# A rope half moved to VectorE, GpSimd's low weight parts cut in two, and eight products moved behind the last softmax steps

## The chip, the cores and the metric

The kernel runs on one core of one Trainium2 chip. A core has a matrix engine (TensorE, PE in the profile, with its weight loads as PEld), three engines for elementwise work (VectorE or DVE, ScalarE or ACT, GpSimd or POOL) and SyncE (SP), which here only issues DMAs. The metric is the device time of one execution in microseconds, taken as the median of several runs.

## The reference

Two layers over 1024 latent tokens of width 1024, with 256 context tokens beside them. All is float32.

```python
# layer 0: windowed attention, 16 query heads, 4 key/value heads of 128
proj = h_lat @ w_in                       # q | k | v | z
q, k = apply_rope(q), apply_rope(k)       # x1*cos - x2*sin, x2*cos + x1*sin
p = softmax([sink, q @ k_ctx.T, q @ k_window.T])   # window of +-128 tokens
y = ((p @ v) * silu(z)) @ w_out
x = x + gate * y
# layer 1: convolution branch, width 2048
a, gl, z = split(h @ w_in + b_in, 3)
u = depthwise_conv(a * sigmoid(gl), 31 taps) + b
y = (silu(layernorm(u)) * silu(z)) @ w_out
out = rmsnorm(x + gate * y) * final_g
```

Ahead of each layer stands a norm with a scale and a shift that are linear in silu(c).

## The kernel before

**High and low parts.** Each float32 product of the projections is made of three faster ones: both operands are split into a rounded high part and the rest, the low part, and high x high, high x low and low x high are added up in PSUM. The high part is a copy by ScalarE, the low part a subtraction (`split_lo`, line 163) by VectorE or GpSimd. A weight chunk is 128x1024: eight blocks of 128x128. The class `WStream` (line 219) loads the chunks in their order (`load`), splits them (`split`, line 239) and hands them out. There are two such streams: `wsA` (line 295) for the 40 chunks of the attention's input projection, `wsB` (line 1414) for the 48 of the convolution's. `wsB` is built with `hp=True`, so that its splits carry a high priority, and gives every low part that isn't VectorE's by a rule of its own (`lo_eng`) to GpSimd: 32 of 48. In `wsA` a low part by GpSimd is already made in two halves of 128x512.

**The order of the work.** TensorE runs its instructions in the order of the program; on the other engines a planner orders them by priority, which falls along the program, and by when it expects the inputs to be there. Each engine then works its queue strictly in order, and waits where an instruction's input is missing.

**The attention.** The softmax goes by pairs of heads and by steps: `steps` holds 8 pairs x 16 steps, a step being 64 queries of both heads. In step i TensorE makes the scores of step i+1 (`scores`, line 1140), then some products from a queue of other work (`fill`, line 1126), then the transposes of step i's probabilities (`transposes`, line 1185). Every fourth step adds products of probabilities with values (`pv`, line 1205). Between the scores and the transposes lie a masking reduction on VectorE, an exponential on ScalarE, a reciprocal on VectorE (tile `sc`) and a scaling on GpSimd (tile `p_page`). Transposed probabilities are split into high and low (tile `pt`) by ScalarE and VectorE.

What `fill` takes is generators of projections, each of which yields after every product: the other query heads and gates; first in the queue is head 1 of the queries (`second_q`, line 1090), last, in the final pair's steps from the eighth on, the first rows of the attention's output projection (`early_proj`, line 923: 7 rows x 2 token blocks x 6 products). `LAST_FILL` (line 40) says how many products a step of the final pair takes: the first number for its steps 0 to 7, the second for 8 to 15. After the last step a loop takes up to 12 more ahead of each product with values that is still due, and then all that is left (lines 1366 on). Before the first scores 18 and then 48 products have been taken, and so all 48 of `second_q`.

**The rope.** `rope` (line 951) takes a projected half of 512 tokens out of PSUM: a copy by ScalarE, two DMAs that swap its partition halves, a product with the cosine by VectorE, a product of the swapped copy with the sine, an addition, a high part by ScalarE and a low part. With `quick`, the sine product, and by `finish` (line 1005) also the addition and the low part, are VectorE's, else GpSimd's. `second_q` calls it for the query half 0 with `quick` and for the half 1 without. Half 0 serves the steps 0 to 7 of the first pair, half 1 the steps 8 to 15.

**Behind the attention.** `proj_attn` (line 761) multiplies by the output weights, in four quarters of the output; the last three rows of the last quarter go block by block, and each block is read out of PSUM by `evac0` (line 868) as soon as it is done: times the gate, plus x, the square's sum on ScalarE, the mean and its inverse root on VectorE (tiles `ms`, `sq`, `rr`, `rq`), scaling. Meanwhile the first chunks of `wsB` are split. In the convolution layer (`b_mm`, line 1647) TensorE makes the three projections; the 31 taps are shared between VectorE (even taps and sums) and ScalarE with GpSimd (odd taps). The layer's mean is a product with a tile of sums (`vsum_page`).

Of the kernel before, what the change touches and what calls it, by code (L numbers as in the profile page):

```python
# [18 lines left out]
KT = D // P  # L19
# [17 lines left out]
FIRST = 5  # L37
EARLY_ROWS = 7
EARLY_AT = 8
LAST_FILL = (11, 10)  # L40
FIRST_FILL = 48
KEEP = 8
BYBLOCK = 3
# [53 lines left out]
def backbone_kernel(  # L97
# [8 lines left out]
    V, A, G, PE, SY = (InOrder(tc, e) for e in (nc.vector, nc.scalar, nc.gpsimd, nc.tensor, nc.sync))  # L106
# [32 lines left out]
    def ps_g():  # L139
        return ps.tile([P, 512], F32, tag="g", name=nm("psg"), bufs=2)  # L140
# [13 lines left out]
    def act(out, in_, func, **kw):  # L154
        return A.activation(out=out, in_=in_, func=func, **kw)

    def tt(eng, out, a, b, op):
        return eng.tensor_tensor(out=out, in0=a, in1=b, op=op)

    def stt(out, in0, scalar, in1, op0, op1):  # L160
        return V.scalar_tensor_tensor(out=out, in0=in0, scalar=scalar, in1=in1, op0=op0, op1=op1)

    def split_lo(eng, lo, full, hi):
        return tt(eng, lo, full, hi.bitcast(F32), ALU.subtract)
# [54 lines left out]
    class WStream:  # L219
# [19 lines left out]
        def split(self, between=None):  # L239
            if self.ns >= self.nl:  # L240
                return
            i = self.ns
            r = self.raw.pop(i)
            h, l = pg.alloc(F32R, [KT, P], "whi"), pg.alloc(F32R, [KT, P], "wlo")
            if self.hp:
                with tc.high_priority():
                    act(h, r, AF.Copy)
                    split_lo(self.lo_eng(i), l, r, h)
            else:
                act(h, r, AF.Copy)  # L250
                if between:
                    between()
                if self.lo_eng(i) is G:
                    for a in range(0, KT, KT // 2):
                        split_lo(G, *(t[:, a:a + KT // 2] for t in (l, r, h)))
                else:
                    split_lo(self.lo_eng(i), l, r, h)
            pg.free(r)
            self.hl[i] = (h, l)
            self.ns += 1  # L260
# [147 lines left out]
    def ada_mm(kt):  # L408

        o = ps_o(0)[:, 0:256]  # L410
        for i in range(2):
            for k in range(4):
                PE.matmul(o[32 * k:32 * k + 32], c32[:, 4 * i + k, :], araw[kt][i][:, k], start=i == 0, stop=i == 1,
                          tile_position=(0, 32 * k))
        pg.free(*araw.pop(kt))
        if kt == KT - 1:
            pg.free(c32)
        return o
# [117 lines left out]
    o = ada_mm(0)  # L536
# [100 lines left out]
    def vt_split(vf, n, dh, dl):  # L637

        tp = ps_o(*vbank)
        for i in range(n // P):  # L640
            PE.transpose(tp[:, i * P:(i + 1) * P], vf[:, i * P:(i + 1) * P], ident)
        t3 = tp[:, 0:n].rearrange("p (a b) -> p a b", b=P)
        act(dh, t3, AF.Copy)
        split_lo(V, dl, t3, dh)
# [116 lines left out]
    def proj_attn():  # L761
# [38 lines left out]
        def ahead(i, nl, ns):  # L800
            while todo["load"] <= min(i + nl, len(seqB) - 1):
                load(todo["load"])
                todo["load"] += 1
            while todo["split"] <= min(i + ns, len(seqB) - 1):
                split(todo["split"])
                todo["split"] += 1
# [124 lines left out]
    qt = {}  # L931
    zt = {}

    def gemm_half(wc, half, o):
        wh, wl = wc
        sl = slice(half * 512, half * 512 + 512)
        for kt in range(KT):
            PE.matmul(o, wh[:, kt], Hh[kt][:, sl], start=kt == 0, stop=False)
            yield
            PE.matmul(o, wh[:, kt], Hl[kt][:, sl], start=False, stop=False)  # L940
            yield
            PE.matmul(o, wl[:, kt], Hh[kt][:, sl], start=False, stop=kt == KT - 1)
            yield

    def by_pairs(ap):
        return ap.rearrange("p (s t) -> p s t", t=64)

    def in_pair(page, n):
        return page.rearrange("p (s e t) -> p s e t", e=2, t=64)[:, :, n % 2]
# [55 lines left out]
    def finish(kind, n, half, o, d, ropes=None, hold=None, quick=False):  # L1005

        sl = slice(half * 512, half * 512 + 512)
        if kind in "kv" and half == 2:
            c = kvt[n][2]
            if kind == "k":  # L1010
                act(c[:, 0], o[:, 0:CT], AF.Copy)
                i = split_lo(V, c[:, 1], o[:, 0:CT], c[:, 0])
                while hold:
                    hold.pop()(i)
                return None
        if kind in "qk":
            return rope(o, sl, d, ropes, hold, V if quick or kind == "q" and half and n and n % 4 == 0 else G,
                        n if kind == "q" else None, quick)
        if kind == "z":
            dv, ov = in_pair(d, n), by_pairs(o)  # L1020
            anchor_z[:] = [act(dv, ov, AF.Tanh, scale=0.5), stt(dv, dv, 1.0, ov, ALU.add, ALU.mult)]
            return None
        w = CT if half == 2 else 512
        f = hp.alloc(F32, None, "vf")
        act(f[:, 0:w], o[:, 0:w], AF.Copy)

        def tail():
            if half == 2:
                vt_split(f, CT, *(c[:, i].rearrange("p (a b) -> p a b", b=P) for i in (2, 3)))
            else:  # L1030
                vt_split(f, 512, *(t[:, half * 4:half * 4 + 4] for t in d))
            hp.free(f)

        return tail
# [50 lines left out]
    def split_next(i):  # L1085
        if wsA.ns <= i:
            wsA.split()
            wsA.load()

    def second_q():  # L1090
        i = cidx[("q", 1)]
        wc = wsA.need(i)
        wsA.load()
        for half in range(2):
            o = ps_g()
            yield from gemm_half(wc, half, o)
            if half == 0:
                split_next(i + 1)
            finish("q", 1, half, o, qt[(0, half)], quick=half == 0)
        wsA.done(i)  # L1100

    def pair_job(kind, pr, half):
# [203 lines left out]
    def next_pv():  # L1306
        pr, qq = pvq.popleft()
        fill(1000, ("z", pr, qq // 2))
        pv(pr, qq)

    fillq.append(("q1", second_q()))
    enqueue_pairs(0)
    fill(18)
# [6 lines left out]
    for i, (pr, st) in enumerate(steps):  # L1320
        h, qb = 2 * pr + st // 8, st % 8
# [15 lines left out]
        if not regroup:  # L1337
            n = 15 if pr and pr % 2 == 0 and st < 4 and not final else LAST_FILL[st // 8] if final else FILL - (i < 6)
            if pr // 2 in vlate and pr:
# [667 lines left out]
```

## Time and profile before

| What | Value |
|---|---|
| median of the runs | 1678.72 us |
| runs | 1678.7 to 1679.17 us |
| the profiled execution | 1680.83 us |
| its span, first to last instruction | 1679.1 us |
| granted TensorE clock, mean | 0.999 |
| busy: TensorE, VectorE, ScalarE, GpSimd | 1666.0, 1091.2, 870.2, 874.9 us |

The profile is of one execution, which is a little longer than the runs; it is read for where time lies, and a difference found in it is applied to the median. A row of the timeline reads: start and duration in us, engine, instruction, output<-inputs by the tiles' names, shape, count, and in brackets how long the engine had stood before it and what ended that. A count over 1 means that alike neighbours were merged into one row, whose duration is theirs together. TensorE's products overlap: one that is listed with 0.39 us lets the next start 0.23 us behind it, so that a stall is read from the starts. A row of the grouped view gives the count, then the busy time of all in us and the mean of one in ns, then the idle time ahead of them. All instructions of the kernel carry the line of a helper (L91), so the tiles tell them apart.

### The profile page before, as it was taken

Reading aid. Unit: us, or ns where it says so; the run is one execution under the profiler, and the core shown is the slowest. Engines: PE = TensorE matmul, PEld = TensorE weight load, DVE = VectorE, ACT = ScalarE, POOL = GpSimd, SP = SyncE. Lnnn points to the kernel's source line nnn. Section 1 sums busy time; section 2 is a strip of 40 time slices with the busy share of each in tenths; the row PEclk is TensorE's granted clock in tenths of the full one; section 3 lists DMA queues with packets and bytes.
Section 4 is the critical chain, followed back from the end, with each engine's and each line's share of the span. In section 5 each row is a group of like instructions: output and inputs, shape, how many; then the busy total and the mean of one; then the engine's idle time right before and its main releaser. Section 6 shows DMA issues by size and latency. Waiting matters only on the chain.

```text
span 1679.1 us, 23843 instructions
## 1 busy us (share of the span) xinstructions
PE 1666.0 (99%) x8340; PEld 1396.3 (83%) x8340; DVE 1091.2 (65%) x2063; ACT 870.2 (52%) x1523; POOL 874.9 (52%) x831
## 2 busy tenths in 40 slices
PE   9999999999999999999999999999999999999998
PEld 6888888888888888888888788888888888888886
DVE  5755554555455554556234389999999999868832
ACT  5644543555355544546333365555665664566731
POOL 0246673576547564642001268999898887130400
PEclk9999999999999999999999999999999999999999
DMA  9424442444335443457976522020211212387981
GB/s 382 171 62 144 141 144 76 142 154 151 105 125 167 148 129 98 127 159 262 325 247 215 193 88 101 1 76 14 76 50 51 88 38 70 132 276 246 318 288 50
DMA packets 139607, 244.63 MB, mean 146 GB/s; under 512 B 44650, under 2 KB 61346, under 8 KB 139488
## 3 DMA queue, kind: packets, MB, share of 16 engines
q1 hardware_dynamic: 133408, 233.15, 40.7%
q10 hardware_dynamic: 6080, 9.97, 2.4%
q8 instruction: 65, 1.06, 0.2%
q14 instruction: 54, 0.44, 0.1%
HBM read 190.90 MB, written 41.69 MB: 139 GB/s over the span
## 4 chain that ended last, share of the span: by engine, by line
PE 97%; DVE 1%; DMA 1%; POOL 0%; ACT 0%; issue 0%; ACTq 0%; POOLq 0%; DVEq 0%
PE psg L91 50%; PE pss L91 26%; PE pso L91 22%; DMA rope_half<-rope_half 1%; POOL rope_half L91 0%; DVE rq L91 0%; DVE x_page L91 0%; DVE ms L91 0%; DVE rope_half L91 0%; POOL kl_page L91 0%; DVE wlo_page L91 0%; ACT whi_page L91 0%; ACTq L91 0%; ACT rope_half L91 0%; DVE hf_page L91 0%
## 5 line engine op out<-in xcount | busy, mean ns | idle before, releaser
L91 POOL TENSOR_TENSOR odd_half<-odd_half,prod_half 128x513 f32<-128x513 f32 (+2 forms) x252 | 314.5, 1256 | 22.5 <-ACT prod_half L91 9.2
L91 POOL TENSOR_TENSOR wlo_page<-wraw_page,whi_page 128x512 fp32r<-128x512 f32 (+1 forms) x104 | 174.9, 1698 | 157.2 <-ACT whi_page L91 125.7
L91 PE MATMUL psg<-hh_page,whi_page 128*128 128x512 f32 x600 | 236.8, 395 | 0.0
L91 PE MATMUL psg<-hl_page,whi_page 128*128 128x512 f32 x600 | 234.8, 391 | 0.0
L91 PE MATMUL psg<-hh_page,wlo_page 128*128 128x512 f32 x600 | 234.3, 390 | 0.0
L91 ACT ACTIVATE prod_half<-ubuf,dww 128x513 f32<-128x513 f32 (+2 forms) x252 | 165.6, 675 | 116.7 <-POOL odd_half L91 113.0
L91 PE MATMUL psg<-h2h_page,whi_page 128*128 128x512 f32 x464 | 181.9, 392 | 0.0
L91 PE MATMUL psg<-h2h_page,wlo_page 128*128 128x512 f32 x464 | 180.6, 389 | 0.0
L91 PE MATMUL psg<-h2l_page,whi_page 128*128 128x512 f32 x464 | 180.6, 389 | 0.0
L91 DVE SCALAR_TENSOR_TENSOR pss<-ubuf,dww,pss 128x512 f32<-128x512 f32 (+3 forms) x270 | 173.0, 674 | 0.1
L91 DVE SCALAR_TENSOR_TENSOR pss<-ubuf,wsum,pss 128x512 f32<-128x512 f32 (+3 forms) x270 | 172.3, 674 | 0.2
L91 ACT ACTIVATE pt<-pss 128x640 fp32r<-128x640 f32 (+1 forms) x128 | 86.7, 677 | 142.5 <-PE pss L91 142.5
L91 POOL TENSOR_SCALAR p_page<-p_page,sc 128x576 f32<-128x576 f32 (+2 forms) x128 | 93.2, 728 | 106.9 <-DVE sc L91 104.4
L91 ACT ACTIVATE p_page<-p_page,sc 128x577 f32<-128x577 f32 (+2 forms) x128 | 96.9, 757 | 78.6 <-DVE sc L91 76.7
L91 DVE CUSTOM_DVE_ANT_0 p_page<-pss,mask_page,nsink 128x576 f32<-128x576 f32 (+1 forms) x112 | 90.2, 806 | 70.5 <-PE pss L91 57.4
L91 PEld LDWEIGHTS psg<-hh_page,wlo_page 128*128 128x128 f32 x600 | 112.7, 188 | 24.2
L91 PEld LDWEIGHTS psg<-hh_page,whi_page 128*128 128x128 f32 x600 | 112.7, 188 | 19.7 <-ACT hh_page L91 0.3
L91 PEld LDWEIGHTS psg<-hl_page,whi_page 128*128 128x128 f32 x600 | 113.0, 188 | 19.1 <-DVE hl_page L91 0.2
L91 DVE TENSOR_TENSOR pt<-pss,pt 128x640 fp32r<-128x640 f32 (+1 forms) x128 | 100.7, 787 | 36.3 <-ACT pt L91 36.1
L91 ACT ACTIVATE whi_page<-wraw_page 128x1024 fp32r<-128x1024 f32 x88 | 92.6, 1052 | 53.9 <-PE psg L91 19.3
L91 PE MATMUL pso<-h2h_page,whi_page 128*128 128x512 f32 x304 | 118.3, 389 | 0.0
L91 PE MATMUL pso<-h2l_page,whi_page 128*128 128x512 f32 x304 | 118.3, 389 | 0.0
(255 smaller groups left out, 3915.6 us busy)
## 6 DMA issues: line engine op xcount, KB each, us to landing
wraw_page<-in_k_wconv_dram SPq DMA_DIRECT2D x48, 512.0 KB
wraw_page<-in_k_win_dram SPq DMA_DIRECT2D x40, 512.0 KB
wo_page<-in_attn_w_out_dram SPq DMA_DIRECT2D x32, 512.0 KB
wol_page<-wolA SPq DMA_DIRECT2D x32, 512.0 KB
wo_page<-in_conv_w_out_dram SPq DMA_DIRECT2D x32, 512.0 KB
wol_page<-wolC SPq DMA_DIRECT2D x32, 512.0 KB
rope_half<-rope_half ACTq DMA_DIRECT2D x76, 128.0 KB
araw_page<-in_k_ada_dram SPq DMA_DIRECT2D x16, 512.0 KB
```

Of the source, the lines that this page charges most:

```text
L91: r = f(*a, **k)
```

## The change

Three places. The second half of head 1's rope is called with `quick=True` too, so that its sine product, its addition and its low part are VectorE's. In streams with `hp=True`, which is `wsB` alone, a low part by GpSimd is made by two instructions of 128x512 instead of one of 128x1024; those by VectorE stay whole. In the final pair's steps 8 to 15, `fill` is asked for 9 products instead of 10.

```diff
@@ -37,7 +37,7 @@
-LAST_FILL = (11, 10)
+LAST_FILL = (11, 9)
@@ -245,7 +245,9 @@
             if self.hp:
                 with tc.high_priority():
                     act(h, r, AF.Copy)
-                    split_lo(self.lo_eng(i), l, r, h)
+                    n = KT // 2 if self.lo_eng(i) is G else KT
+                    for a in range(0, KT, n):
+                        split_lo(self.lo_eng(i), *(t[:, a:a + n] for t in (l, r, h)))
@@ -1096,7 +1098,7 @@
             yield from gemm_half(wc, half, o)
             if half == 0:
                 split_next(i + 1)
-            finish("q", 1, half, o, qt[(0, half)], quick=half == 0)
+            finish("q", 1, half, o, qt[(0, half)], quick=True)
```

## The prediction

> **What bounds the kernel now.** I read the page's head and its chain by engine first, then TensorE's rows in order of time for every place where two products start further apart than they need to, then the rows of the other engines around those places.
>
> ```profile
> span 1679.1 us, 23843 instructions
> PE 1666.0 (99%) x8340; PEld 1396.3 (83%) x8340; DVE 1091.2 (65%) x2063; ACT 870.2 (52%) x1523; POOL 874.9 (52%) x831
> PE 97%; DVE 1%; DMA 1%; POOL 0%; ACT 0%; issue 0%; ACTq 0%; POOLq 0%; DVEq 0%
> 1023.81 5.44 PE pso L91 x24
> ```
>
> TensorE is busy for 99% of the span and holds 97% of the chain. The last row, from the chain, gives the pace of an undisturbed 128x512 product: 5.44/24 = 0.227 us. The change takes no product away, so all that it can win is time in which TensorE stands. Three such places lie where the change works; I call them A, B and C. A is the first softmax step:
>
> ```profile
> 94.35 0.39 PE L91 MATMUL psg<-hl_page,whi_page 128*128 128x512 f32 x1
> 96.31 0.66 PE L91 MATMUL pss<-ident,p_page 128*128 128x128 f32 x4 [1.58 <-POOL p_page L91]
> ...
> 93.00 1.29 POOL L91 TENSOR_TENSOR rope_half<-rope_half,sin_page 128x512 f32<-128x512 f32 x1 [5.92 <-DMA rope_half<-rope_half]
> 94.38 1.27 POOL L91 TENSOR_TENSOR rope_half<-rope_half,rope_half 128x512 f32<-128x512 f32 x1
> 95.62 1.31 POOL L91 TENSOR_SCALAR p_page<-p_page,sc 128x448 f32<-128x448 f32 x2
> ...
> 88.04 0.69 DVE L91 TENSOR_TENSOR rope_half<-rope_half,rope_half 128x512 f32<-128x512 f32 x1
> 91.56 0.68 DVE L91 CUSTOM_DVE_ANT_1 p_page<-pss,mask_page,nsink 128x448 f32<-128x448 f32 x1 [0.84 <-PE pss L91]
> 93.25 0.17 DVE L91 RECIPROCAL sc<-sc 128x1 f32<-128x1 f32 x1 [0.22 <-ACT p_page L91]
> 96.83 0.69 DVE L91 SCALAR_TENSOR_TENSOR zs_page<-zs_page,psg 128x512 f32<-128x512 f32 x1 [2.71 <-ACT zs_page L91]
> ...
> 90.51 2.36 DMA rope_half<-rope_half
> ```
>
> TensorE could have gone on at 94.35 + 0.23 = 94.58 and goes on at 96.31: it stands for 1.73 us. The transposes wait for GpSimd's scaling of the first probabilities. Its factor is there at 93.42 (the reciprocal), but GpSimd's queue holds the rope of head 1's second query half ahead of it, which waits for a transfer that lands at 92.87 and then takes two additions' time, to 95.65.
>
> B is the end of the attention's output projection:
>
> ```profile
> 959.84 0.39 PE L91 MATMUL pss<-woh_page,ozl_page 128*128 128x512 f32 x1
> 961.25 0.50 PE L91 MATMUL pss<-woh_page,ozh_page 128*128 128x512 f32 x1 [1.01 <-DVE x_page L91]
> ...
> 952.69 7.68 POOL L91 TENSOR_TENSOR wlo_page<-wraw_page,whi_page 128x1024 fp32r<-128x1024 f32 x3 [28.89 <-DMA wraw_page<-in_k_wconv_dram]
> ...
> 952.83 2.82 DVE L91 TENSOR_TENSOR x_page<-x_page,xr_page 128x512 f32<-128x512 f32 x1
> 956.44 1.49 DVE L91 SCALAR_TENSOR_TENSOR ms<-ssf 128x1 f32<-128x1 f32 x1 [0.79 <-ACT junk_half L91]
> 958.40 2.00 DVE L91 SCALAR_TENSOR_TENSOR rq<-rr 128x1 f32<-128x1 f32 x1
> 960.43 0.16 DVE L91 TENSOR_TENSOR rq<-rq,ms 128x1 f32<-128x1 f32 x1
> 960.50 0.69 DVE L91 TENSOR_TENSOR x_page<-pss,gate_page 128x512 f32<-128x512 f32 x1
> ...
> 955.68 0.63 ACT L91 ACTIVATE junk_half<-x_page 128x512 f32<-128x512 f32 x1 [1.79 <-DVE x_page L91]
> 956.31 1.05 ACT L91 ACTIVATE whi_page<-wraw_page 128x1024 fp32r<-128x1024 f32 x1
> ```
>
> Here TensorE stands for 961.25 - 959.84 - 0.23 = 1.18 us, until VectorE has read block 1 out of PSUM (960.50). That read sits in VectorE's queue behind block 0's norm, and three instructions of that norm are swollen: the addition takes 2.82 where the rope's of the same shape takes 0.69, and two instructions on a single column take 1.49 and 2.00 where their sibling takes 0.16. GpSimd runs three whole low parts just then, 952.69 to 960.37, some 2.5 us each, and the swollen instructions end at 955.65, 957.93 and 960.40, about where a third of that row does each time.
>
> C is the last softmax step, before its value products:
>
> ```profile
> 798.81 0.60 PE L91 MATMUL pss<-ident,p_page 128*128 128x128 f32 x4
> 800.18 0.47 PE L91 MATMUL pso<-pt,kvc_page 128*128 128x512 f32 x1
> 800.88 1.43 PE L91 MATMUL pso<-pt,kvc_page 128*128 128x512 f32 x5 [0.23 <-DVE pt L91]
> ...
> 799.50 0.60 ACT L91 ACTIVATE pt<-pss 128x512 fp32r<-128x512 f32 x1 [2.22 <-PE pss L91]
> 800.13 0.69 DVE L91 TENSOR_TENSOR pt<-pss,pt 128x512 fp32r<-128x512 f32 x1 [2.12 <-ACT pt L91]
> ```
>
> TensorE stands for 800.88 - 800.18 - 0.23 = 0.47 us for the low part of the transposed probabilities. A, B and C together are 3.38 us: the most that I can name.
>
> **The rope on VectorE.** Three instructions leave GpSimd (sine product, addition, low part) for VectorE, which does the first half's addition in 0.69. They add 2.07 us to an engine that idles for 2.71 just behind. No DMA is added; the swap is issued by ScalarE as before. The products of this half are first read eight steps later, so only what the three displace counts. Where they stand in VectorE's queue isn't in the trace. If the two reciprocals keep their place, scaling starts at 93.45, ends at 94.1 (half of 1.31), before TensorE wants it: gain 1.73. If, as on GpSimd today, product and addition stand ahead of the reciprocal, they run 92.9 to 94.3; reciprocal to 94.5, scaling to 95.15, TensorE at 95.2: gain 1.1. If the product stands ahead of the score reduction, VectorE waits for the landing with the reduction behind it, which then starts at 94.3 instead of 91.56; reduction to scaled probabilities takes 91.56 to 93.42 plus 0.65 = 2.5, so TensorE goes at 96.85: a loss of 0.5. I take 1.1, because on GpSimd the addition was put ahead of the scaling. Next late would be the second step's scaling, which the last GpSimd row (x2) shows right behind the first and which moves forward with it.
>
> **The halves.** 32 low parts of 128x1024 become 64 of 128x512. The grouped rows give both shapes:
>
> ```profile
> L91 POOL TENSOR_TENSOR wlo_page<-wraw_page,whi_page 128x512 fp32r<-128x512 f32 x72 | 94.9, 1341 | 90.1 <-ACT whi_page L91 89.2 <-POOL p_page L91 0.5 <-PE pss L91 0.3
> L91 POOL TENSOR_TENSOR wlo_page<-wraw_page,whi_page 128x1024 fp32r<-128x1024 f32 x32 | 80.1, 2504 | 67.1 <-ACT whi_page L91 36.5 <-DMA wraw_page<-in_k_wconv_dram 28.9 <-PE psg L91 1.7
> ```
>
> GpSimd pays 2 x 1.341 - 2.504 = 0.18 us more for each, 5.7 in all; no weight is waited for at B or behind it, so that lies beside TensorE's work. At B I replay the queue with halves of 1.25. The addition (issued 952.83) gets through at 953.94 and ends at 954.55, 1.1 sooner. Square and its sum on ScalarE to 955.35; the mean waits for the second half, done by 955.95; the root stands behind a weight copy of 1.05 on ScalarE, 956.65; the reciprocal to 956.85; the next instruction waits for the third half, done 957.35; its successor, free today, may be caught by the fourth, done 958.75. Block 1 is then read by 959.45, and TensorE wants the bank at 960.07: all of 1.18 goes, with 0.6 to spare. If mean and both that follow are each caught for a whole half (1.25 + 0.16), they end at 956.75, 958.65 and 960.1, block 1 is read by 960.8 and 0.5 is won; and if the last one is caught by the very last half, which may end at 961.4 (the present 960.37 with three extra costs of 0.18 and the addition's share let in), B costs up to 1 us more than now. I take 1.18, since the first term alone nearly covers it. The Trainium skill ("SBUF — State Buffer", section "Who interferes with whom") says that a VectorE instruction with two SBUF inputs and a GpSimd instruction that reads SBUF exclude each other for the whole instruction, by order of issue. By that rule twice as many GpSimd instructions are twice as many chances to be caught, and B would give the 0.5; the swollen rows agree that a wait ends with GpSimd's instruction, and show three caught beside three low parts.
>
> **Nine early products.** Eight steps give up one product each; the early projection has 7 rows x 2 blocks x 6 = 84 products, so 72 stand in the steps (80 before) and 12 behind the last transposes (4 before), which is what the closing loop takes at once. At C the transposes start at 798.81 and the low part is done at 800.82, 2.0 later. From the transposes to the first value product lie 1.37 with four products, 0.91 of it theirs; with twelve it is 0.46 + 12 x 0.227 = 3.2: covered, 0.47 won. The price is 0.23 us less cover in each of the steps. Only one has as little:
>
> ```profile
> 780.19 0.75 POOL L91 TENSOR_SCALAR p_page<-p_page,sc 128x576 f32<-128x576 f32 x1 [1.67 <-DVE sc L91]
> 781.18 0.71 PE L91 MATMUL pss<-ident,p_page 128*128 128x128 f32 x5
> ```
>
> 780.94 against 781.18: 0.24 of cover for 0.23. I cost it at nothing; if the order there is worse, up to 0.4 stays behind.
>
> The sum: 1.1 + 1.18 + 0.47 = 2.75, near 2.8. The profiled execution took 1680.83, its span is 1679.1, so 1.7 lies around it, untouched; 1680.83 - 2.8 = 1678.0. The median, 1678.72, is 2.1 lower than that execution, and the gain is one of stalls that each execution should have: 1678.72 - 2.8 = 1675.9.
>
> **The rivals.** First, all three stalls go in full: 3.38, 1675.3. For it: VectorE's idle 2.71 behind the reciprocals; against it, GpSimd's order today.
>
> Second, the rope blocks VectorE ahead of the first score reduction: -0.5 + 1.18 + 0.47 = 1.15, 1677.6. For it, the product ranks ahead of the scores in the program's order; against it, the reduction is ready at 91.56, well before the landing.
>
> Third, the halves don't do what they are there for, because as many of VectorE's small instructions are caught: 1.1 + 0.47 = 1.6, 1677.1.
>
> Fourth, slower. In the convolution both engines are nearly full and VectorE's last sum is only just in time, as the timelines and the grouped rows of that stage show:
>
> ```profile
> 1432.59 0.69 DVE L91 TENSOR_TENSOR vsum_page<-vsum_page,v_page 128x512 f32<-128x512 f32 x1
> 1434.38 1.02 PE L91 MATMUL pso<-vsum_page,ones 128*128 128x512 f32 x2
> ...
> L91 DVE TENSOR_TENSOR wlo_page<-wraw_page,whi_page 128x1024 fp32r<-128x1024 f32 x13 | 20.4, 1572 | 5.4 <-ACT whi_page L91 4.5 <-issue 0.5
> L91 DVE TENSOR_TENSOR vsum_page<-vsum_page,v_page 128x1024 f32<-128x1024 f32 x13 | 20.4, 1570 | 0.0
> ...
> 1023.68 1.23 DVE L91 TENSOR_TENSOR wlo_page<-wraw_page,whi_page 128x1024 fp32r<-128x1024 f32 x1
> ```
>
> The sum ends at 1433.28, TensorE reads it at 1434.38: 1.1 us of cover at the end of the whole stage. VectorE's 26 wide instructions with two SBUF inputs already take 0.34 longer than a free one (1.57 against 1.23), 8.9 us. Were more GpSimd instructions to double that, VectorE would be 8.9 - 1.1 = 7.8 late there: 1678.72 - 2.8 + 7.8 = 1683.7. It decides from 1.1 us on. Against it: low parts are few beside the odd taps' additions on GpSimd, and each is caught for less time once it is short.
>
> **How the numbers follow.** Forecast 0.45, all in full 0.22, rope ahead of the reduction 0.13, halves without effect 0.12, convolution late 0.08. A measurement here can tell about 0.2% from no change, 3.4 us, so faster means under 1675.4: the case in full (0.22), and some of the forecast's (0.06), 0.28. Slower is the fourth rival and a little of the unknown at B, 0.09; the rest, 0.63, is within. The range goes from 1675.3 less the 0.5 by which the runs shown differ, 1674.8, to 1677.6 plus the same, 1678.1; the slow case is left out.
>
> **What would show it.** A: transposes of the first step at 95.2 (forecast) or 94.6, no rope of that half on GpSimd at 93, and the reciprocal behind or ahead of the addition on VectorE. B: the 2.82, 1.49 and 2.00 each shorter by a microsecond, and no wait in the last block of the projection. C: 12 products between the last transposes and the value products, and no wait there. The convolution: the last sum still ahead of TensorE's mean. The forecast is wrong if a new wait of over 0.5 us stands in the softmax steps from the eighth of the last pair on, or at the mean.

## The result, and the profile after

| | before | after |
|---|---|---|
| median | 1679.05 us (8 runs) | 1683.51 us (8 runs) |
| ratio | 1 | 1.0027, 95% interval 1.0016 to 1.0038 |
| the profiled execution | 1680.83 us, span 1679.1 | 1682.3 us, span 1680.2 |
| mean granted TensorE clock | 0.999 in the profiled execution | 0.996 to 0.999 |

The three runs behind the 1678.72 of before are among its eight here. The granted clock is the share of its full speed that TensorE is given. The changed kernel is slower by 4.5 us; the forecast was 2.8 us faster, with a range that ended at 1678.1. The busy times on the page after, and its chain by engine:

```profile
PE 1665.3 (99%) x8340; PEld 1395.6 (83%) x8340; DVE 1088.1 (65%) x2066; ACT 869.7 (52%) x1523; POOL 876.1 (52%) x860
PE 95%; DMA 2%; DVE 1%; POOL 1%; ACT 1%; issue 0%; ACTq 0%; POOLq 0%; DVEq 0%; SPq 0%
```

TensorE is as busy as before (1665.3 against 1666.0), and TensorE's share of the chain falls from 97% to 95%: the time is lost in stands. The rows of the timeline after that answer to those of A:

```profile
93.51 0.39 PE L91 MATMUL psg<-hl_page,whi_page 128*128 128x512 f32 x1
97.17 0.65 PE L91 MATMUL pss<-ident,p_page 128*128 128x128 f32 x4 [3.27 <-POOL p_page L91]
...
92.02 0.69 DVE L91 TENSOR_TENSOR rope_half<-rope_half,sin_page 128x512 f32<-128x512 f32 x1 [2.24 <-DMA rope_half<-rope_half]
92.75 0.69 DVE L91 TENSOR_TENSOR rope_half<-rope_half,rope_half 128x512 f32<-128x512 f32 x1
93.36 0.68 DVE L91 CUSTOM_DVE_ANT_1 p_page<-pss,mask_page,nsink 128x448 f32<-128x448 f32 x1
96.21 0.16 DVE L91 RECIPROCAL sc<-sc 128x1 f32<-128x1 f32 x1 [0.89 <-ACT p_page L91]
...
93.47 0.63 ACT L91 ACTIVATE qh_page<-rope_half 128x512 fp32r<-128x512 f32 x1 [4.44 <-DVE rope_half L91]
94.12 1.28 ACT L91 ACT_TABLE_LOAD   x1
95.41 0.67 ACT L91 ACTIVATE p_page<-p_page,sc 128x449 f32<-128x449 f32 x1
...
96.47 1.39 POOL L91 TENSOR_SCALAR p_page<-p_page,sc 128x448 f32<-128x448 f32 x2 [10.31 <-DVE sc L91]
```

A is twice as long: 97.17 - 93.51 - 0.23 = 3.43 us for 1.73. GpSimd is free now and scales at once, but its factor comes at 96.37. VectorE's queue holds the sine product ahead of the first score reduction and waits 2.24 us in it for the swapped copy; the product and the addition then go first, and the reduction starts at 93.36, though its scores were there from about 90.7 (91.56 before, and TensorE is 0.84 earlier here, 93.51 for 94.35). On ScalarE the high part of the rope stands ahead of the load of the exponential's table. The timeline of before has that load in an idle time, and the rope's high part behind the exponentials:

```profile
91.15 1.28 ACT L91 ACT_TABLE_LOAD   x1 [1.18 <-issue]
92.45 0.67 ACT L91 ACTIVATE p_page<-p_page,sc 128x449 f32<-128x449 f32 x1
95.68 0.63 ACT L91 ACTIVATE qh_page<-rope_half 128x512 fp32r<-128x512 f32 x1 [1.76 <-POOL rope_half L91]
```

So the exponential starts 2.05 us behind the reduction now (95.41 - 93.36), and before 0.89 (92.45 - 91.56).

The rows that answer to B and C, and one place that is new:

```profile
955.14 0.69 DVE L91 TENSOR_TENSOR x_page<-x_page,xr_page 128x512 f32<-128x512 f32 x1
957.28 0.98 DVE L91 SCALAR_TENSOR_TENSOR ms<-ssf 128x1 f32<-128x1 f32 x1 [1.44 <-ACT junk_half L91]
959.65 1.11 DVE L91 SCALAR_TENSOR_TENSOR rq<-rr 128x1 f32<-128x1 f32 x1
960.68 0.68 DVE L91 TENSOR_TENSOR x_page<-pss,gate_page 128x512 f32<-128x512 f32 x1
...
798.83 0.60 PE L91 MATMUL pss<-ident,p_page 128*128 128x128 f32 x4
801.83 0.39 PE L91 MATMUL psg<-woh_page,ozl_page 128*128 128x512 f32 x1
802.05 1.52 PE L91 MATMUL pso<-pt,kvc_page 128*128 128x512 f32 x6
...
813.92 0.39 PE L91 MATMUL pss<-woh_page,ozl_page 128*128 128x512 f32 x1
815.25 0.68 PE L91 MATMUL pso<-ident,dwr_page 32*128 32x32 f32 x8 [0.94 <-DVE dww L91]
```

B's wait is gone: block 1 is read at 960.68 and no product of the last block waits. Of the three swollen instructions the last two are shorter (0.98 and 1.11 for 1.49 and 2.00), but the first, the addition, isn't caught at all, that is, it doesn't wait for GpSimd: 0.69, not a shortened 2.82. The two shorter ones are not the halves' doing either: in a run further down that has whole low parts and an addition that isn't caught (e8) they take 0.83 and 0.96. So this trace doesn't show yet what the halves do. C is gone: the value products follow 0.22 us behind the last of the twelve. One place is worse: at 815.25 TensorE stands for 1.1 us (815.25 - 813.92 - 0.23) at the transposes of the convolution's taps, where before it didn't. The chain of waits after says why:

```profile
799.50 13.09 DMA ozf_page<-ozd
812.68 1.07 ACT ozh_page L91
813.77 1.23 DVE ozl_page L91
```

VectorE's copy of the first taps, whose bank the next transposes need, stands in its queue behind the low part of the last attention rows (the row DVE ozl), whose transfer lands at 812.6. Before, that transfer was issued at the same time (799.47), and ScalarE's high part of it started at 807.82 instead of 812.68.

Of the profiled executions, then: A 1.7 worse, B 1.18 and C 0.47 better, the taps 1.1 worse. That is about what the spans differ by (1.1), and not the 4.5 of the medians. The mean clocks say that something is missing: this profiled execution, at 0.999, is the fastest of the eight; four of the eight have a mean clock of 0.997 or less. Of the 127 runs of before that stand beside the experiments two have: one at 0.997, and one that took 2078 us and, like one of e3's and one of e7's at over 4300 us, enters no ratio.

### The profile page after: what moved, and what is told of

The parts are those of the page before. It is cut to its first block, busy times and chain, and to the rows that moved or that the text cites. A ratio compares the mean times of both kernels' runs of the same rounds, so it can differ in the third digit from the quotient of the medians.

```text
span 1680.2 us, 23876 instructions
## 1 busy us (share of the span) xinstructions
PE 1665.3 (99%) x8340; PEld 1395.6 (83%) x8340; DVE 1088.1 (65%) x2066; ACT 869.7 (52%) x1523; POOL 876.1 (52%) x860
## 3 DMA queue, kind: packets, MB, share of 16 engines
q8 instruction: 65, 1.06, 0.3%
## 4 chain that ended last, share of the span: by engine, by line
PE 95%; DMA 2%; DVE 1%; POOL 1%; ACT 1%; issue 0%; ACTq 0%; POOLq 0%; DVEq 0%; SPq 0%
PE psg L91 49%; PE pss L91 25%; PE pso L91 21%; DMA rope_half<-rope_half 1%; DMA ozf_page<-ozd 1%; DMA wolA<-low_page 1%; POOL rope_half L91 0%; POOL low_page L91 0%; ACT whi_page L91 0%; DVE rope_half L91 0%; ACTq L91 0%; POOL p_page L91 0%; ACT rope_half L91 0%; ACT qh_page L91 0%; DVE x_page L91 0%
## 5 line engine op out<-in xcount | busy, mean ns | idle before, releaser
L91 POOL TENSOR_TENSOR wlo_page<-wraw_page,whi_page 128x512 fp32r<-128x512 f32 x136 | 180.2, 1347 | 154.2 <-ACT whi_page L91 122.8
```

The costliest lines, as they stand in the source:

```text
L91: r = f(*a, **k)
```

## The experiments

Theory Q: the rope's place in the queues of VectorE and ScalarE is the loss. The first rival was that the nine products, through the taps' transposes, or the halves cost as much. (The expectations of e1 to e4 call the theory R and this rival Q; from e5 on the theory is Q.) Every kernel was timed beside runs of before; the medians of before lie between 1679.72 and 1679.80.

| kernel | median, us | ratio to before, 95% interval | stand at A in its trace |
|---|---|---|---|
| rope alone (e1) | 1683.80 | 1.0021, 1.0012 to 1.0030 | 3.68 |
| halves alone (e2) | 1679.62 | 0.9998, 0.9989 to 1.0007 | 1.92 |
| nine alone (e3) | 1679.85 | 1.0001, 0.9992 to 1.0010 | 1.92 |
| halves and nine, no rope (e4) | 1679.78 | 1.0001, 0.9992 to 1.0010 | 1.50 |
| rope alone, behind the softmax (e5) | 1678.27 | 0.9990, 0.9981 to 0.9999 | 0 |
| rope alone, table loaded early (e6) | 1681.65 | 1.0012, 1.0003 to 1.0021 | 1.86 |
| rope alone, 15 more products at A (e7) | 1678.03 | 0.9987, 0.9978 to 0.9996 | 0.28 |
| before, 8 more products at A (e8) | 1677.99 | 0.9989, 0.9980 to 0.9997 | 0 |
| before, 4 fewer at A (e9) | 1684.64 | 1.0028, 1.0017 to 1.0039 | 2.66 |
| before, 9 fewer at A (e10) | 1683.91 | 1.0027, 1.0018 to 1.0037 | 3.69 |
| before, 3 fewer in the last step (e11) | 1678.46 | 0.9994, 0.9985 to 1.0003 | 1.85 |
| e8, halves and e11 together (e12) | 1677.05 | 0.9985, 0.9976 to 0.9994 | 0 |
| the whole change, rope behind the softmax (e13) | 1678.38 | 0.9989, 0.9980 to 0.9998 | 0 |
| the changed kernel again (e14) | 1683.65 | 1.0018, 1.0009 to 1.0026 | 3.39 |
| before, block 0's addition later (e15) | 1680.83 | 1.0003, 0.9994 to 1.0012 | 1.46 |
| halves, block 0's addition later (e16) | 1679.29 | 0.9994, 0.9985 to 1.0002 | 2.08 |

**The parts by themselves.** e4 holds the edits of e2 and e3 together.

```diff
 e1
-            finish("q", 1, half, o, qt[(0, half)], quick=half == 0)
+            finish("q", 1, half, o, qt[(0, half)], quick=True)
 e2
-                    split_lo(self.lo_eng(i), l, r, h)
+                    n = KT // 2 if self.lo_eng(i) is G else KT
+                    for a in range(0, KT, n):
+                        split_lo(self.lo_eng(i), *(t[:, a:a + n] for t in (l, r, h)))
 e3
-LAST_FILL = (11, 10)
+LAST_FILL = (11, 9)
```

> The rope alone. Theory R (the rope is the loss): on VectorE its product and addition stand ahead of the first score reduction, and on ScalarE its high part ahead of the load of the exponential's table, so TensorE stands 3.4 us instead of 1.7 at the first transposes; the stall alone makes 1.7 us more than the kernel before (ratio 1.001). The change's median is 4.5 us above and its executions had a lower mean clock than the profiled one; if a stand of that length also lowers TensorE's clock for a while, this run shows it too and is 3 to 5 us slower (1.002 to 1.003). Rival Q (the loss comes from transfers and queues that the other two edits reorder): 1.7 us at most and the spread of the kernel before.

> The halves alone. Theory R: 1.2 to 1.3 us faster than the kernel before (ratio 0.9992): the stall of 1.18 at the end of the output projection is gone and nothing else changes by over 0.3. Rival Q: the reordered queues take it back, 0 to 2 us slower. The stall of 1.73 at the first transposes stays in both.

> The nine products alone. Theory R: the stall of 0.47 ahead of the last value products is gone, 0.5 us faster (ratio 0.9997). Rival Q: the stall of 1.1 us at the transposes of the convolution's taps and 0.2 in the last pair's first step with 9 products, which the changed kernel has, are from this edit: 0.8 us slower (1.0005), with the load of the gate rows issued some 13 us later than before and the last row of the early projection's neighbour landing late.

> Halves and nine products, without the rope. Theory R: faster than the kernel before by 0.5 to 1.8 us (ratio 0.9990 to 0.9997), 3 to 5 us faster than the change. Rival Q: within 1 us of the changed kernel less 1.7, thus 1 to 3 us slower than before (1.0006 to 1.002).

The rope by itself costs 4.0 us, the two other parts nothing that shows, alone or together. The theory's forecasts for e2 and e4, some 1.2 and 0.5 to 1.8 us faster, were missed as well: 0.2 and nothing. But the rival can't make up the 4.5, and the question became why the rope costs more than the 1.7 that its stand has grown by. In the timeline of e1 the scores right behind A are longer than any such row so far:

```profile
99.10 0.62 PE L91 MATMUL pss<-kh_page,qh_page 128*128 128x320 f32 x1
```

They take 0.62 us, where the row of the same scores behind A takes 0.39 in the trace of after (at 97.58). The stand ahead of them is 3.68 us, and the clock record has 3.41 us at half speed from its end on. That gave theory C: a stand of over 3.4 us lets the granted clock fall to half. The profiled execution after, with 3.43 us and no half clock behind it, lay at its very edge.

**The place of the rope (e5), the table (e6), cover (e7, e8).**

```diff
 e5, in rope; other lines hand "later" through for half 1 alone and run it behind the scores of step 1
-        if ropes is None:
+        if ropes is None and later is None:
             tt(V if quick else G, w, w, sin[:, sl], ALU.mult)
...
+        elif later is not None:
+            later.append(lambda: (after(tt(V, w, w, sin[:, sl], ALU.mult), anchor_r), add(), low()))
 e6, in second_q
+            if half == 0:
+                act(small([P, 1], name="early", bufs=1), o[:, 0:1], AF.Exp, scale=0.0)
 e7, on e1
-FILL - (i < 6)
+FILL - (i < 15) + 15 * (i == 0)
 e8, on before
+FILL - (i < 6) + 8 * (i == 0)
```

> The rope alone on VectorE (no halves, no nine), but its sine product, addition and low part emitted behind the scores of step 1, the sine product tied behind the reciprocal of step 1. VectorE's order is then both reductions, both reciprocals, sine product, gate's product, addition, and ScalarE's high part comes behind both exponentials. Theory Q (the loss is the place in the queues: reduction behind the sine product's DMA, exponential's table load behind the high part): the stand at A goes from 3.7 us with the rope alone to below 0.4 us, no half clock behind it, and the kernel is about 1.7 us faster than before (ratio 0.999; 1678.1 against 1679.8). Rival V (it is VectorE's three more instructions as such, wherever they stand): a stand of 1 us or more stays in the steps 0 to 3 and the time is at or over before's.

> The rope alone on VectorE, where the change puts it, and one exponential of a single column on ScalarE behind the copy of head 1's first half, so that the table load stands in an idle time of ScalarE instead of in front of the first exponential. Theory Q: 1.28 us of the stand of 3.7 us are the table load; about 2.1 to 2.4 us stay (reduction behind the sine product). Theory C (a stand of over 3.4 us lets the granted clock fall to half for the next 3.4 us): no half clock here, since the stand is shorter, so the time falls by more than the 1.3, by 2 to 2.5 us, to about before's or 0.5 over (ratio 1.000 to 1.0004). Rival to C (the clock has nothing to do with the stand): half clock still there behind A in the record or the time falls by 1.3 alone, to 1682.4.

> The rope alone on VectorE, where the change puts it, but TensorE is given 15 more products (3.4 us) in the first softmax step, and one fewer in the steps 6 to 14. Nothing is done about the queues: reduction, exponential and scaling stay as late as with the rope alone. Theory Q with C: the stand at A shrinks to 0.2 to 0.5 us, no half clock behind it, the time is 1 to 1.7 us below before's (1678.1 to 1678.8). Rival V (the delay is handed on to the second and third step, whose reductions stand behind the same queue): a stand of over 1 us turns up in steps 1 to 3, and the time stays above before's.

> The kernel before with 8 more products (1.8 us) in the first softmax step, nothing else changed; the first pair's later products run out that much earlier. Theory: the stand of 1.73 us at A is TensorE's alone and is won whole, 1.7 us (1678.1 against 1679.8, ratio 0.999). Rival: the products are missing later in the pair, where gate and query halves are due, and a stand of the same size turns up there: 1679.8.

e5 does all the work that e1 does, on the same engines, and is 1.5 us faster than before where e1 is 4.0 slower. Its timeline at A:

```profile
91.45 0.68 DVE L91 CUSTOM_DVE_ANT_1 p_page<-pss,mask_page,nsink 128x448 f32<-128x448 f32 x1 [0.69 <-PE pss L91]
93.28 0.16 DVE L91 RECIPROCAL sc<-sc 128x1 f32<-128x1 f32 x1 [0.36 <-ACT p_page L91]
94.07 0.69 DVE L91 TENSOR_TENSOR rope_half<-rope_half,sin_page 128x512 f32<-128x512 f32 x1
...
94.25 0.39 PE L91 MATMUL psg<-hl_page,whi_page 128*128 128x512 f32 x1
94.48 0.60 PE L91 MATMUL pss<-ident,p_page 128*128 128x128 f32 x4
```

The reduction starts when the scores are there, the sine product fills VectorE's idle time behind the reciprocals, and the transposes follow 0.23 behind the last product: the gain of 1.73 that the prediction named as the best case. Rival V (three more instructions on VectorE cost, wherever they stand) is out.

e6 is a mixed result. The exponential follows the high part directly and A shrinks to 1.86 us, but the little exponential itself holds a bank that TensorE wants next, as its timeline shows:

```profile
87.22 0.50 PE L91 MATMUL psg<-hh_page,whi_page 128*128 128x512 f32 x1 [0.77 <-ACT early L91]
```

That is a new stand of 0.93 us. Both together are 2.79, 0.9 less than in e1, and 1.06 more than in before. The median fell by 2.15 against e1 and no half clock is in the trace, as theory C has it; against before, 1.9 us remain where the stands explain 1.06; 0.8 stays unexplained. So e6 agrees with C, misses the stand of 2.1 to 2.4 that was expected at A, and doesn't measure the table's 1.28 cleanly.

e7 leaves every queue as late as e1 has it and only gives TensorE 3.4 us of work meanwhile: 1678.03, 5.8 us below e1. So what e1 loses is lost through the stand and what follows from it, and no stand of the size turns up in the later steps. e8 does the same for before and wins A without touching the rope: 1.8 us.

**The clock (e9, e10, e14).** e9 and e10 take products away at A from the kernel before, whose rope stays on GpSimd. e14 is the changed kernel, unaltered.

```diff
 e9
-FILL - (i < 6)
+FILL - (i < 6) - 4 * (i == 0)
 e10
-FILL - (i < 6)
+FILL - (i < 6) - 9 * (i == 0)
```

> The kernel before with 4 products fewer (0.9 us) in the first softmax step, nothing else: the same rope and the same queues, only a longer stand at A, about 1.73 + 0.91 = 2.6 us. Theory C (a stand of over 3.4 us lets the granted clock fall to half for 3.4 us): no half clock, mean clock 0.999 as before, time before's plus 0.9 (1680.7 against 1679.8). Rival to C (any longer stand lowers the clock a little): clock below 0.998 in a third of the runs or more, time plus 1.5 or more.

> The kernel before with 9 products fewer (2.04 us) in the first softmax step, nothing else: a stand at A of about 3.8 us, as long as with the rope on VectorE, but with GpSimd's rope and before's queues. Theory C: half clock for 3.4 us behind A and a mean clock of 0.998 or less in half of the runs or more; the time is before's plus 2.04 for the stand and 1 to 1.7 in the runs that are hit, 1682.5 to 1683.3 in the median. Rival (the low clock of the changed kernel comes from something else in it, such as VectorE's or ScalarE's order): clock 0.999 and 1681.8.

> The changed kernel as it is, beside the others on one chip. Theory: 1683 to 1684.5 as before; if its profiled run has the first half-clock window behind A, the granted clock shows 0.50 for 3.4 us from where the stand ends, and the stand of some 3.4 to 3.7 us fills over 60% of one stretch of 3.4 us; if not, the stand is split over two stretches. Rival (the half clock belongs to the other kernels only): no run at a mean clock of 0.997 or below.

e10 bears out that a long stand brings the half clock, on a kernel with GpSimd's rope: 4.2 us for a stand that is 1.96 longer, where a stretch at half clock costs 1.6 (worked out below); 0.6 stays unexplained, and the median lies as much above the range that was expected. e9 refutes C's threshold: a stand of 2.66 us has half clock behind it too, and the median is up by 4.9, of which 0.93 is the longer stand, some 1.6 the clock, and 1.5 two other waits in its trace (0.85 at 176.80, 0.69 at 229.20); 0.8 stays unexplained. So I read the clock again, in stretches of 3.41 us, which is the step in which all changes of the clock record lie. First e14, then the profiled execution of the changed kernel shown above; the columns are stretch, length, TensorE's busy time with its count, granted clock, DMA share and GB/s:

```profile
93.10:96.51 3.41, 1.28 (x6) 1.00 0.00 0
96.51:99.93 3.42, 2.32 (x10) 0.50 0.00 0
99.93:103.34 3.41, 3.41 (x10) 0.50 0.13 38
103.34:106.75 3.41, 3.41 (x21) 1.00 0.00 0
```

```profile
92.02:95.44 3.42, 1.88 (x9) 1.00 0.00 0
95.44:98.85 3.41, 1.68 (x12) 1.00 0.00 0
```

The stands are alike, 3.39 and 3.43 us. In e14 the stand lies mostly in one stretch, which is left with 1.28 us of work; the clock is at half for the next two, and came back after the first that was busy throughout. In the other execution the stand falls on a boundary, 1.88 and 1.68 us of work are left, and the clock stays. Of the seventeen traces of after and e1 to e16, five have half clock behind A (e1, e9, e10, e14, e16). The one of them with the most work left in a stretch is e16; of the twelve without, e2 is the one with the least:

```profile
93.94:97.35 3.41, 1.49 (x10) 1.00 0.00 0
97.35:100.76 3.41, 3.41 (x12) 0.50 0.15 38
```

```profile
94.04:97.45 3.41, 1.64 (x11) 1.00 0.00 0
```

So what decides in these traces is how much of one such stretch TensorE works: 1.64 of 3.41 us was enough, 1.49 was not. The ends of the kernels agree. In before TensorE works 0.67 us of the stretch from 1670.82 and is at half clock from 1674.23 to its end; in e16 it works 1.64 of the stretch from 1670.90, and the clock stays for one stretch more. The price of a stretch at half clock follows from the starts of products in e14's timeline:

```profile
100.39 0.63 PE L91 MATMUL psg<-hh_page,whi_page 128*128 128x512 f32 x1
100.82 0.63 PE L91 MATMUL psg<-hl_page,whi_page 128*128 128x512 f32 x1
```

They lie 0.427 apart instead of 0.227, so a full stretch loses 3.41 x 0.200 / 0.427 = 1.6 us, and e14's two lose (2.32 + 3.41) x 0.47 = 2.7. Where the stretches lie against the kernel differs between executions of one kernel: in after one begins 1.49 us ahead of the last product before A (92.02 and 93.51), in e14 0.89 (93.10 and 93.99). Six of e14's eleven runs have a mean clock of 0.997 or less (three of them 0.996). That count is a lower bound, since the traces of e1 and e16 list 0.998 with one stretch at half clock. Two runs of e1 list 0.947 and 0.948 at times like the others'; nothing here explains these two figures. The rival, that the half clock belongs to other kernels, is out.

**The halves (e15, e16).** In ten of the traces the low parts are whole, and B's wait is in two of them only. In the two the addition is issued 0.14 and 0.06 us behind GpSimd's first low part (952.83 and 952.69 in before); in the other eight it is issued 0 to 0.20 us ahead of it and takes 0.69. e15 and e16 put two copies of one column ahead of that addition, in before and in e2:

```diff
         tt(V, t, acc, gbc0[0][:, ns], ALU.mult)
+        for _ in range(2 if s == len(subs) - 1 and b == 0 else 0):
+            V.tensor_copy(small([P, 1], name="pause", bufs=2), t[:, 0:1])
```

> The kernel before with two copies of one column on VectorE ahead of block 0's addition in the last quarter (0.3 us), so that the addition starts behind GpSimd's first whole low part in every execution. Theory B (whoever is issued second waits for the other's end): the addition takes 2.6 us or more, the wait at the last block is there, 1.2 to 1.5 us, and the median is 0.7 to 1.2 us above before's 1679.8 (before itself has the wait in some executions). Rival (the swollen addition has another cause): it takes 0.69 and there is no wait.

> The halves alone, with the same two copies ahead of block 0's addition. Theory B with the forecast's replay: the addition is caught by a half and takes 1.3 to 1.9 us; the wait at the last block is gone, and the time is 1.0 to 1.4 us below the one with whole low parts, at 1679.6. Rival (as many small instructions are caught by the next halves): a wait of 0.5 us or more stays.

The timelines, e15 first:

```profile
952.25 2.73 DVE L91 TENSOR_TENSOR x_page<-x_page,xr_page 128x512 f32<-128x512 f32 x1
955.77 1.50 DVE L91 SCALAR_TENSOR_TENSOR ms<-ssf 128x1 f32<-128x1 f32 x1 [0.79 <-ACT junk_half L91]
957.73 1.99 DVE L91 SCALAR_TENSOR_TENSOR rq<-rr 128x1 f32<-128x1 f32 x1
...
952.03 7.67 POOL L91 TENSOR_TENSOR wlo_page<-wraw_page,whi_page 128x1024 fp32r<-128x1024 f32 x3 [29.06 <-DMA wraw_page<-in_k_wconv_dram]
...
960.38 0.50 PE L91 MATMUL pss<-woh_page,ozh_page 128*128 128x512 f32 x1 [0.98 <-DVE rq L91]
```

```profile
955.43 1.65 DVE L91 TENSOR_TENSOR x_page<-x_page,xr_page 128x512 f32<-128x512 f32 x1
957.87 0.38 DVE L91 SCALAR_TENSOR_TENSOR ms<-ssf 128x1 f32<-128x1 f32 x1 [0.79 <-ACT junk_half L91]
959.64 1.10 DVE L91 SCALAR_TENSOR_TENSOR rq<-rr 128x1 f32<-128x1 f32 x1
...
955.23 8.64 POOL L91 TENSOR_TENSOR wlo_page<-wraw_page,whi_page 128x512 fp32r<-128x512 f32 x6 [29.08 <-ACT whi_page L91]
```

With the addition 0.22 us late the three long instructions of the profile before come back one for one (2.73, 1.50, 1.99), and TensorE waits (960.38 - 959.01 - 0.23 = 1.14). With halves they are 1.65, 0.38 and 1.10, and no product waits. The medians lie 1.54 us apart, 1680.83 and 1679.29, and ten of e16's eleven runs lie below e15's median; the two intervals against before overlap, so that the wait in the traces is the stronger sign. So the halves do what they are for, wherever B happens. They also have a price beside TensorE's work: with halves the next small instruction, rq from rq and ms, takes 0.84 in e16 and after where it takes 0.16 in before (960.43), and where the addition isn't caught the norm's instructions are longer with halves (e2: 1.01, 1.10 and 0.85) than with whole low parts (e8: 0.83, 0.96 and 0.16). No product waits for it.

**The last step (e11) and a better kernel (e12, e13).** e11 takes three products from the last step of the kernel before alone. e12 is e8 with the halves and e11, and its rope stays on GpSimd. e13 is the whole change with e5's place for the rope.

```diff
 e11
-LAST_FILL[st // 8] if final
+LAST_FILL[st // 8] - 3 * (st == 15) if final
```

> The kernel before with 7 products instead of 10 in the last softmax step alone, so that 7 instead of 4 stand behind the last transposes. Theory: the wait at C of 0.47 us goes, the order of the queues elsewhere stays, so that the taps' transposes at 813 don't wait for the addition of a DMA that came later, as they do with 9 products in all eight steps (0.8 to 1.1 us): 0.47 us faster than before (1679.3 against 1679.8, too little for a verdict; the trace decides). Rival (the late transfer ahead of the taps' transposes comes with any product moved behind the last transposes): the wait of 0.8 to 1.1 us at the taps' transposes is here too.

> The kernel before with what the runs so far point to: the rope left on GpSimd, 8 more products in the first softmax step (A covered), the low parts in halves (B), and 7 products in the last softmax step (C). Theory: A, B and C all go, 1.7 + 0.5 (B is there in some executions only, taken at half) + 0.47 = 2.7, 1677.1 against 1679.8 (ratio 0.9984). Rival: the halves and the shift of C give nothing that shows, 1678.0 as with the cover alone.

> The whole change, but with the rope of the second half emitted behind the scores of step 1 and its sine product tied behind that step's reciprocal. Theory Q (the rope's place is the whole of the loss): stand at A gone, no half clock, 1678.3 to 1678.9 where before has 1679.8 (the rope's gain of 1.5 to 1.7 as measured alone, halves nothing, the nine products 0.47 won and 0.8 to 1.1 given back); 4 to 5 us below the changed kernel. Rival (the loss needs the three parts together): it stays above before's time.

The timeline of e11, at C and at the taps:

```profile
799.69 1.08 PE L91 MATMUL pso<-pt,kvc_page 128*128 128x512 f32 x4
...
811.57 0.39 PE L91 MATMUL pss<-woh_page,ozl_page 128*128 128x512 f32 x1
811.89 0.68 PE L91 MATMUL pso<-ident,dwr_page 32*128 32x32 f32 x8
```

C is gone with seven products behind the transposes, and the taps' transposes don't wait. With nine products in all eight steps they wait in each of the five traces that have them (0.75 to 1.14 us), and SyncE issues its transfers there in another order than before: the gate's, 512 KB, at 790.49 instead of 777.27. That this order is what makes the last rows' transfer land late is argued, not shown. e11's 1.3 us is inside its interval's noise; the trace decides, by 0.47.

e13 has all that the change has and is 1.4 us faster than before, 5.3 below e14: the rope's place, with the half clock that its stand brings, is the whole loss. e12 is the fastest of all, 2.7 us below before. All the waits of its TensorE that the waits view lists, in us, are these, and they lie in the first 80 us:

```profile
PE pss L91 <- DVE zerr_page L91: 2.0, 1, 2.0
PE pso L91 <- ACT vf_half L91: 0.5, 1, 0.5
PE pss L91 <- DVE hl_page L91: 0.2, 1, 0.2
```

## Why the prediction was wrong, point by point

**The step that failed** is "The rope on VectorE": "I take 1.1, because on GpSimd the addition was put ahead of the scaling." The place that I had put at 0.13, product and addition ahead of the score reduction, is the one that came, and e5 and e13, which differ from e1 and the changed kernel in nothing but this place, win where those lose. GpSimd's order was the wrong row to infer from: there the rope stood ahead of a scaling that wasn't ready, while on VectorE it had to be compared with a reduction that was. Why the planner chose so, most likely because it expected the swapped copy sooner than it lands, is only argued.

**Its price was mis-sized too**, at 0.5 for 1.7. Of the second rival the first half is right: the reduction was put at 94.3 in before's times, and it started at 93.36 after, where TensorE was 0.84 ahead (93.74 against 94.58, the end of its products), which is 94.20. What I took over from before is the way from there to the scaled probabilities, 2.5. It is 1.16 longer, because the rope's fourth instruction, the high part on ScalarE, moved as well: it went ahead of the table load, and with it the 1.28 that had been hidden in ScalarE's idle time came into the path. Two prices, 0.5 and 1.16, are the 1.7. The working counted three instructions that leave GpSimd, and not the one on ScalarE that is fed by them.

**The clock was not thought of.** The sum has no term for it. Another 1.6 us for each stretch at half clock, in at least 10 of the 19 runs of the changed kernel (those at 0.997 or less), comes on top and makes some 4 of 1.7. The profile of before has no half clock behind A, where its stretch keeps 1.84 us of work, but it has one at its end, and nothing was made of it. How near A was to the edge shows in e16, whose rope is before's: there the stand is 2.08 and the clock falls.

**B was the right mechanism and the wrong frequency.** "The gain is one of stalls that each execution should have" was an assumption about one trace. The trace of before happens to be one of two in ten in which the addition is issued a tenth of a microsecond too late; its 1680.83 against a median of 1678.72 may have been a hint, and I took that difference to lie elsewhere. Taken at 2 in 10, the term is 0.24 and not 1.18. The replay itself holds: it had the addition end 1.72 after its issue, and e16 measures 1.65. The third rival, as many small instructions caught, came in its first half: after the addition three more are longer than alone (0.38, 1.10 and 0.84, where 0.16 is free), but by less than a whole half each, and the wait did not come. By the Trainium skill ("SBUF — State Buffer", section "Who interferes with whom") the two instructions exclude each other in order of issue. The rows of e15 agree: issued 0.22 behind, the addition ends 0.39 behind where a third of GpSimd's row does.

**C was right, and given back.** The 0.47 was won by the twelve products as worked out. The price was worked out from the cover of each step and put at nothing; what was missed is that with a product taken out of each of eight steps the order of SyncE's transfers is another too, and that a wait of 0.75 to 1.14 at the taps comes with it. The convolution's last sum kept its place: the fourth rival's cover at the mean is 1.1 us after as well, and that rival, which had the right sign, had the wrong place; that its 1683.7 is 0.2 from what was measured is luck.

The sum as it came out, from the first profiled execution against the forecast: A +1.7 for -1.1, B -0.2 in the mean for -1.18, C and the taps +0.6 for -0.47, half clock +1.6 to +2.7 in most executions for nothing. That is 3.7 to 4.8 in an execution that has the half clock; 4.5 and 3.9 were measured.

## What to carry to other kernels

Before work is moved to a less busy engine, write down what stands behind it in that engine's queue, and in the queue of every engine that takes up its result: a strict queue turns a wait for a transfer into a wait for everybody behind it, and work that was hidden in an idle time (here a table load) can be pushed out of it. A stall that is read from one trace is one draw; if two engines' issue times differ by a tenth of a microsecond there, ask for a second trace before the gain is counted. Where TensorE is the bound, independent products moved into the gap (e8, eight of them) are worth as much as moving the late work (1.8 us against e5's 1.5), and no stand showed elsewhere for it.

## What the hardware showed that was not expected

A gap of 2.08 us in TensorE's work was enough to halve the granted clock for the next 3.41 us, and one of 3.43 was not, depending on where the gap fell against a fixed grid of 3.41 us: with 1.49 us or less of work in a stretch the clock fell, with 1.64 or more it stayed, and it came back after a stretch at half clock that was busy throughout or nearly so (3.28 of 3.41 in e10 was enough, 2.32 in e14 was not). Each stretch costs 1.6 us. The Trainium skill ("TensorE: Matmul & The Clock Gate", Part 1) tells of a free-running window of 3413 ns after which an idle array is clocked at half; the length and the half agree with these traces. Its section "HAM oscillation" sums that up as no gaps over some 3.4 us; here the measurement decides for a lower bound, since e9's 2.66 and e16's 2.08 were hit.

The mutual exclusion of VectorE and GpSimd lets 0.06 us decide over 2 us: the same addition takes 0.69 when it is issued just ahead of GpSimd's whole low part and 2.73 to 2.89 when it is issued just behind. It works both ways: GpSimd's first low part takes 2.85 where it is issued behind the addition (e8), and 2.41 where it is ahead (before).
